# RG-LRU gates: two matmul products in place of three, on operands stacked by 64-channel block

## The chip, the cores and the metric

The kernel runs on one core of a Trainium2 chip. The metric is the device time of one execution in microseconds; of several runs the median is taken.

## The reference

One layer of a diffusion backbone: 1024 latent tokens and 256 context tokens of width 1024. A norm and one wide projection feed two branches, a bidirectional RG-LRU and a bidirectional mLSTM; they are projected, gated, merged and added to the stream, and a SwiGLU layer and a last norm follow. The change touches only the RG-LRU's gates. Each direction d has two of them, r (weights `wa`) and i (weights `wx`), made by 16 blocks of 64 x 64 on the 1024 channels:

```python
def _rglru_coeffs(xc, wa, ba, wx, bx, lam):
    r = jax.nn.sigmoid(_block_diag(xc, wa) + ba).astype(jnp.float32)
    i = jax.nn.sigmoid(_block_diag(xc, wx) + bx).astype(jnp.float32)
    log_a = -RG_C * jax.nn.softplus(-lam.astype(jnp.float32)) * r
    a = jnp.exp(log_a)
    b = jnp.sqrt(-jnp.expm1(2.0 * log_a)) * (i * xc.astype(jnp.float32))
    return a, b
```

`xc` is the projection after a convolution of four taps over the tokens. A linear scan with a and b follows, forward and backward.

## The kernel before

Channels lie on the 128 partitions, tokens in columns. Matmul operands are float32 numbers split into a high part (rounded to fp32r) and the rest, the low part, and each product is made as three matmuls: high x high, high x low, low x high (`gemm`, L107 to 117).

The RG-LRU stage (L671 to 831) handles the channels in eight tiles of 128, that is two blocks of 64 each. A step of its loop (m = 0 to 7) does three things on TensorE: the projection of the next tile m+1 in eight pieces A[0] to A[7] (one per 128 input channels, nine matmuls each, two of 512 latent columns and one of 256 context columns per product), the four gates of tile m (`gate`, L724), and the projection of m's gelu branch (48 matmuls of 512 columns). In the last step there is no next tile, and the pieces belong to a side projection without context columns (six matmuls each).

A gate q = 2d + j (direction d; j = 0 for r, 1 for i) has 128 x 128 weights with its two blocks on the diagonal and zeros elsewhere. It is made on 1284 columns (256 context, three of padding between, 1024 latent, one more), cut into 512, 512 and 260, each with three matmuls into the accumulator tile `pt`. There is one such tile (`bufs=1`, three banks), so the next gate waits until ScalarE has read it: one sigmoid over 128 partitions x 1284 columns (L734).

The rest of a step, in the order in which the code has it:

- ScalarE: sigmoid and tanh of gate 0, sigmoids of gates 1, 2 and 3, a tanh, copies of the next tile's projection from the accumulators (L687, L688), two roots (L818), two exponentials (L820), rounding of the next tile's high part (`high`, L696), gelu (L827). Tables are loaded ahead of roots, exponentials, gelu and sigmoids.
- VectorE: the `tail` of the tile before (L754: products, scans, sums), two products of i with xc (L796, L804), low parts of weights (L100, L721), the taps (`conv`, L201 and L203), two combinations (L821), the low part of the next tile (`low`, L700).
- GpSimd rounds weights (L97, L720), clears paddings and issues the stores; SP issues the loads.

This order is written out by hand and kept: the loop stands in `tc.manual_schedule(engines=ENG4)` (L779) for TensorE, ScalarE, VectorE and GpSimd, so each of them runs its instructions in the order of the code and stands still where one has to wait. The high part lies in the tile `xh` (one buffer), the low part in a buffer of tag `X` (two). Weights of the gates are packed on the host by `layout`.

Of the kernel before, what the change touches and what calls it, by code (L numbers as in the profile page):

```python
# [17 lines left out]
KT = 8  # L18
EPS = 1e-6
NFF = 22  # L20
LP = 1284
# [21 lines left out]
def hybrid_block(ctx, tc, xT, ctxT, vec, gbias, wmod, wmt, win, wbr, wbm, wo, wfi, wfo, qkvt, wif, rgw,  # L43
# [17 lines left out]
    def V(name, i=0, n=1):  # L61
        o = VEC[name][0] + i
        return vt[:, o:o + n]
# [607 lines left out]
    with pool("p2") as p2, pool("p2t", bufs=1, space=PSUM) as pt_, pool("p2c", bufs=1, space=PSUM) as pc_:  # L671
        PW = 1312

        def wide(tag, bufs, dt=F32, n=LP):
            return p2.tile([128, PW], dt, tag=tag, name=tag, bufs=bufs)[:, 0:n]

        def rg_parts(m, w):

# [15 lines left out]
            def high():  # L694
                got["xh"] = wide("xh", 1, F32R)
                nc.scalar.activation(got["xh"], got["xc"], AF.Identity)  # L696

            def low():
                got["xl"] = wide("X", 2, F32R)
                nc.vector.tensor_tensor(got["xl"], got["xc"], got["xh"].bitcast(F32), op=ALU.subtract)  # L700

# [21 lines left out]

        def gate(m, q, got, rhl):  # L724

            d, j = q // 2, q % 2
            (rh, rl), xh, xl = rhl, got["xh"], got["xl"]
            pt = pt_.tile([128, 1536], F32, tag="gt", name="pt")
            for a, b in ((0, 512), (512, 1024), (1024, LP)):
                nc.tensor.matmul(pt[:, a:b], lhsT=rh[:, q], rhs=xh[:, a:b], start=True, stop=False)  # L730
                nc.tensor.matmul(pt[:, a:b], lhsT=rh[:, q], rhs=xl[:, a:b], start=False, stop=False)
                nc.tensor.matmul(pt[:, a:b], lhsT=rl[:, q], rhs=xh[:, a:b], start=False, stop=True)
            g = wide(f"g{j}", 4)
            nc.scalar.activation(g, pt[:, 0:LP], AF.Sigmoid, bias=V(("ba", "bx")[j], 8 * d + m))  # L734
            return g

        def half_tanh(m, d, r):

            t = wide("t", 3)
            nc.scalar.activation(t, r, AF.Tanh, scale=hsp[:, 8 * d + m:8 * d + m + 1])  # L740
            return t
# [37 lines left out]
        with tc.manual_schedule(engines=ENG4):  # L779
            for m in range(KT):  # L780
# [3 lines left out]
                else:  # L784
                    A, store = side_parts(nw)
                r, t, ii = [None] * 2, [None] * 2, [None] * 2
                A[0]()
                A[1]()
                if before:
                    tail(*before)  # L790
                r[0] = gate(m, 0, got, rhl)
                t[0] = half_tanh(m, 0, r[0])
                A[2]()
                A[3]()
                ii[0] = gate(m, 1, got, rhl)
                nc.vector.tensor_tensor(ii[0], ii[0], got["xc"], op=ALU.mult)  # L796
                w = load_split(win[8 + m])
                A[4]()
                A[5]()
                r[1] = gate(m, 2, got, rhl)  # L800
                A[6]()
                ii[1] = gate(m, 3, got, rhl)
                t[1] = half_tanh(m, 1, r[1])
                nc.vector.tensor_tensor(ii[1], ii[1], got["xc"], op=ALU.mult)  # L804
                if more:
# [741 lines left out]
def layout(inputs):  # L1547
# [38 lines left out]
    for j, n in enumerate(("ml_wi", "ml_wf")):  # L1586
        for d in range(2):
            o = 8 * j + 4 * d
            wif[:, :, :, o:o + 4] = f[n][0, d].reshape(3, KT, 128, 4).transpose(2, 0, 1, 3)
    rgw = np.zeros((128, KT, 4, 128), np.float32)  # L1590
    for d in range(2):
        for j, n in enumerate(("rg_wa", "rg_wx")):
            w = f[n][0, d].reshape(KT, 2, 64, 64)
            for b in range(2):
                rgw[64 * b:64 * b + 64, :, 2 * d + j, 64 * b:64 * b + 64] = w[:, b].transpose(1, 0, 2)
    s = np.arange(128)
# [40 lines left out]
```

## Time and profile before

| what | value |
|---|---|
| median of 3 runs | 1857.31 us (1856.84 to 1858.59) |
| the profiled execution | 1857.61 us, span 1855.8 us |
| TensorE busy | 1828.0 us, 98% of the span |
| TensorE weight loads | 1511.5 us, 81% |
| VectorE busy | 1191.1 us, 64% |
| ScalarE busy | 631.1 us, 34% |
| GpSimd busy | 325.0 us, 18% |
| mean granted TensorE clock | 0.997 |
| chain that ended last | 93% TensorE, 5% VectorE, 1% ScalarE, 1% issue |

The profile is one execution taken by the hardware profiler. The span runs from the first to the last instruction. An engine's idle time in front of an instruction is given in brackets with what ended it. Matmuls overlap in their records, so how long a group of them takes is read from start to start. The RG-LRU stage begins at about 225 us and its loop ends at about 480.

### The profile page before, as it was taken

The page shows a single profiled execution, that of the slowest core. Times are in us where ns is not written, and L with a number is a line of the kernel's source. Part 1 is how long each engine was busy: PE and PEld are TensorE (multiplying, and loading weights), DVE is VectorE, ACT ScalarE, POOL GpSimd, SP SyncE. Part 2 cuts the span into 40 slices and gives each one's busy share as a digit, 9 for nine tenths or more (in the row PEclk, how much of TensorE's full clock was granted, in tenths as well). Part 3 has the DMA queues.
Part 4 walks back from the last instruction along what each step waited for, and adds up shares of the span by engine and source line. Part 5 has one row for each costly group of instructions (what it writes and reads, how often), then busy time and mean ns, then how long its engine had stood idle before and what let it go on. Part 6 is the DMA issues. An engine that isn't in the chain of part 4 may idle for free.

```text
span 1855.8 us, 22833 instructions
## 1 busy us (share of the span) xinstructions
PE 1828.0 (98%) x8850; PEld 1511.5 (81%) x8850; DVE 1191.1 (64%) x1717; ACT 631.1 (34%) x902; POOL 325.0 (18%) x444
## 2 busy tenths in 40 slices
PE   7899999999999999999999999999999999999997
PEld 5778788888888888888888888888888888888887
DVE  6875669889526363636676446787855555687756
ACT  5432357576333232323200012543333333210013
POOL 1121110110134343434101022110000000110003
PEclk9999999999999999999999999999999999999999
DMA  8242211111543333332786443343422222642102
GB/s 349 84 154 94 84 52 57 52 65 50 187 111 73 121 85 109 88 106 79 282 320 215 138 158 136 137 148 131 156 83 80 85 75 108 243 168 99 57 1 91
DMA packets 89364, 227.75 MB, mean 123 GB/s; under 512 B 8073, under 2 KB 37289, under 8 KB 89129
## 3 DMA queue, kind: packets, MB, share of 16 engines
q1 hardware_dynamic: 75864, 179.74, 29.1%
q0 software_dynamic: 12688, 46.17, 6.5%
q8 instruction: 69, 1.13, 0.3%
q10 hardware_dynamic: 704, 0.40, 0.1%
q14 instruction: 39, 0.31, 0.1%
HBM read 175.85 MB, written 50.43 MB: 122 GB/s over the span
## 4 chain that ended last, share of the span: by engine, by line
PE 93%; DVE 5%; ACT 1%; issue 1%; DMA 0%; SPq 0%; POOL 0%; DVEq 0%; ACTq 0%
PE pg L115 12%; PE pg L113 12%; PE pg L117 12%; PE pp L1179 7%; PE pp L1181 7%; PE pp L1180 7%; PE pp L1457 4%; PE pp L1459 4%; PE pp L1458 4%; PE pC L957 3%; PE po L951 2%; PE po L113 2%; PE po L115 2%; PE po L117 2%; PE po L949 1%; PE pt L730 1%
## 5 line engine op out<-in xcount | busy, mean ns | idle before, releaser
L115 PE MATMUL pg<-al,wh 128*128 128x512 f32 x896 | 281.9, 395 | 5.3 <-DVE al L362 3.5
L113 PE MATMUL pg<-ah,wh 128*128 128x512 f32 x896 | 282.8, 396 | 2.9 <-ACT ah L340 1.7
L117 PE MATMUL pg<-ah,wl 128*128 128x512 f32 x896 | 279.5, 393 | 0.0
L97 POOL TENSOR_SCALAR wh<-wr 128x1024 fp32r<-128x1024 f32 x102 | 112.2, 1103 | 614.8 <-PE pg L115 222.5
L100 DVE TENSOR_TENSOR wl<-wr,wh 128x1024 fp32r<-128x1024 f32 x102 | 126.6, 1243 | 120.8 <-POOL wh L97 120.1
L115 PEld LDWEIGHTS pg<-al,wh 128*128 128x128 f32 x896 | 164.3, 189 | 40.3 <-DVE al L362 3.9
L117 PEld LDWEIGHTS pg<-ah,wl 128*128 128x128 f32 x896 | 165.0, 189 | 33.9
L113 PEld LDWEIGHTS pg<-ah,wh 128*128 128x128 f32 x896 | 162.7, 189 | 35.7 <-issue 4.5
L1457 PE MATMUL pp<-hh,wh 128*128 128x512 f32 (+1 forms) x384 | 144.4, 376 | 0.0
L1458 PE MATMUL pp<-hh,wh 128*128 128x512 f32 (+1 forms) x384 | 144.1, 375 | 0.0
L1459 PE MATMUL pp<-hh,wl 128*128 128x512 f32 (+1 forms) x384 | 144.1, 375 | 0.0
L1471 DVE SCALAR_TENSOR_TENSOR xs<-pp,g,xs 128x512 f32<-128x512 f32 x144 | 105.5, 746 | 48.0 <-PE pp L1459 45.3
L1179 PE MATMUL pp<-th,oh 128*128 128x512 f32 x264 | 102.8, 389 | 0.0
L1181 PE MATMUL pp<-th,ol 128*128 128x512 f32 x264 | 102.7, 389 | 0.0
L1180 PE MATMUL pp<-tl,oh 128*128 128x512 f32 x264 | 102.7, 389 | 0.0
L1191 DVE TENSOR_TENSOR c<-c,pp 128x512 f32<-128x512 f32 x84 | 57.4, 683 | 69.5 <-PE pp L1181 52.1
L1226 ACT ACTIVATE oh<-os 128x512 fp32r<-128x512 f32 x88 | 55.3, 632 | 133.1 <-PE pp L1180 103.1
L962 DVE SCALAR_TENSOR_TENSOR Cn<-Cn,decs,pC 128x257 f32<-128x257 f32 x128 | 57.6, 477 | 46.6 <-PE pC L957 46.6
L1405 POOL DMA_DIRECT2D s_h<-c x44 | 23.9, 543 | 361.8 <-DVE c L1404 338.3
L1459 PEld LDWEIGHTS pp<-hh,wl 128*128 128x128 f32 x384 | 72.3, 188 | 14.0
L1457 PEld LDWEIGHTS pp<-hh,wh 128*128 128x128 f32 x384 | 72.3, 188 | 13.9
L1458 PEld LDWEIGHTS pp<-hh,wh 128*128 128x128 f32 x384 | 72.3, 188 | 13.9
(350 smaller groups left out, 3754.1 us busy)
## 6 DMA issues: line engine op xcount, KB each, us to landing
wr<-in_wfi SPq DMA_DIRECT2D x53, 512.0 KB, 3.4
wr<-in_win SPq DMA_DIRECT2D x48, 512.0 KB, 3.4
wr<-in_wmt SPq DMA_DIRECT2D x32, 512.0 KB, 4.8
s_h<-c POOLq DMA_DIRECT2D x44, 256.0 KB, 2.5
wr<-in_wfo SPq DMA_DIRECT2D x22, 512.0 KB, 4.3
g<-s_h SPq DMA_DIRECT2D x22, 512.0 KB, 4.6
wm<-in_wmod SPq DMA_DIRECT2D x16, 512.0 KB, 7.9
wr<-in_wo SPq DMA_DIRECT2D x16, 512.0 KB, 3.4
```

The lines of the kernel that those rows point to most:

```text
L97: nc.gpsimd.tensor_scalar(h, r, 1.0, 0.0, op0=ALU.mult, op1=ALU.add)
L100: nc.vector.tensor_tensor(l, r, h.bitcast(F32), op=ALU.subtract)
L113: nc.tensor.matmul(o, lhsT=wh[:, k], rhs=h(k), start=f, stop=False)
L115: nc.tensor.matmul(o, lhsT=wh[:, k], rhs=l(k), start=False, stop=False)
L117: nc.tensor.matmul(o, lhsT=wl[:, k], rhs=h(k), start=False, stop=e)
L1179: nc.tensor.matmul(o, lhsT=wh(k), rhs=bh(k), start=new and k == 0, stop=False, skip_group_check=True)
L1180: nc.tensor.matmul(o, lhsT=wh(k), rhs=bl(k), start=False, stop=False, skip_group_check=True)
L1181: nc.tensor.matmul(o, lhsT=wl(k), rhs=bh(k), start=False, stop=not more and k == n - 1, skip_group_check=True)
L1457: nc.tensor.matmul(po, lhsT=wh[:, m], rhs=hh[:, sl], start=i == 0, stop=False)
L1458: nc.tensor.matmul(po, lhsT=wh[:, m], rhs=hl[:, sl], start=False, stop=False)
L1459: nc.tensor.matmul(po, lhsT=wl[:, m], rhs=hh[:, sl], start=False, stop=i == n - 1)
L1471: nc.vector.scalar_tensor_tensor(xs[:, m, sls[t]], po, g2[:, m:m + 1], xs[:, m, sls[t]], op0=ALU.mult, op1=ALU.add)
```

## The change

For each block b of a tile one operand z[b] of 128 partitions is made: the block's 64 channels in their high part on the block's own partitions, and the same 64 channels in their low part on the other 64. `high` and `low` therefore write two half tiles each, in place of one whole tile; a half of `low` reads the partitions of one block and writes those of the other.

The weights are packed anew: for direction d and block b, both halves of the 128 rows hold the same 64 x 64 weights, `wa` in columns 0 to 63 and `wx` in 64 to 127. One matmul with the high part of these weights thus adds the products with the high and with the low part of the block, and a second one with the low part of the weights adds the rest (and low x low, which was left out before). A call of `gates(m, d, b)` makes r and i of one block with six matmuls, in place of nine for one gate of two blocks. r is on partitions 0 to 63 of `pt` and i on 64 to 127, so each call is read by two sigmoids of 64 partitions x 1284 columns.

There are still four such calls in a step. They stand after A[0], A[2], A[4] and A[6] now; the four gates stood after A[1], A[3], A[5] and A[6]. The first tanh, the first product with xc and the load of the gelu weights follow the second call.

```diff
@@ -674,6 +674,8 @@
         def wide(tag, bufs, dt=F32, n=LP):
             return p2.tile([128, PW], dt, tag=tag, name=tag, bufs=bufs)[:, 0:n]
 
+        BLK = [(0, slice(0, 64)), (1, slice(64, 128))]
+
         def rg_parts(m, w):
 
             pg = pg_.tile([128, 2, 512], F32, tag="g", name="pg")
@@ -692,12 +694,15 @@
                 conv(got["xc"], got["X"], "rgcw", "rgcb", m)
 
             def high():
-                got["xh"] = wide("xh", 1, F32R)
-                nc.scalar.activation(got["xh"], got["xc"], AF.Identity)
+
+                got["z"] = [wide("xh", 1, F32R), wide("X", 2, F32R)]
+                for b, o in BLK:
+                    nc.scalar.activation(got["z"][b][o], got["xc"][o], AF.Identity)
 
             def low():
-                got["xl"] = wide("X", 2, F32R)
-                nc.vector.tensor_tensor(got["xl"], got["xc"], got["xh"].bitcast(F32), op=ALU.subtract)
+                for b, o in BLK:
+                    z = got["z"][b]
+                    nc.vector.tensor_tensor(z[BLK[1 - b][1]], got["xc"][o], z[o].bitcast(F32), op=ALU.subtract)
 
             return [lambda k=k: gemm(w, movs, [k]) for k in range(KT)], copies, taps, high, low, got
 
@@ -721,18 +726,17 @@
             nc.vector.tensor_tensor(rl, rw, rh.bitcast(F32), op=ALU.subtract)
             return rh, rl
 
-        def gate(m, q, got, rhl):
-
-            d, j = q // 2, q % 2
-            (rh, rl), xh, xl = rhl, got["xh"], got["xl"]
+        def gates(m, d, b, got, rhl, outs):
+
+            (rh, rl), z, o = rhl, got["z"][b], BLK[b][1]
             pt = pt_.tile([128, 1536], F32, tag="gt", name="pt")
-            for a, b in ((0, 512), (512, 1024), (1024, LP)):
-                nc.tensor.matmul(pt[:, a:b], lhsT=rh[:, q], rhs=xh[:, a:b], start=True, stop=False)
-                nc.tensor.matmul(pt[:, a:b], lhsT=rh[:, q], rhs=xl[:, a:b], start=False, stop=False)
-                nc.tensor.matmul(pt[:, a:b], lhsT=rl[:, q], rhs=xh[:, a:b], start=False, stop=True)
-            g = wide(f"g{j}", 4)
-            nc.scalar.activation(g, pt[:, 0:LP], AF.Sigmoid, bias=V(("ba", "bx")[j], 8 * d + m))
-            return g
+            for a, e in ((0, 512), (512, 1024), (1024, LP)):
+                nc.tensor.matmul(pt[:, a:e], lhsT=rh[:, 2 * d + b], rhs=z[:, a:e], start=True, stop=False)
+                nc.tensor.matmul(pt[:, a:e], lhsT=rl[:, 2 * d + b], rhs=z[:, a:e], start=False, stop=True)
+            for j in range(2):
+                if b == 0:
+                    outs.append(wide(f"g{j}", 4))
+                nc.scalar.activation(outs[j][o], pt[BLK[j][1], 0:LP], AF.Sigmoid, bias=V(("ba", "bx")[j], 8 * d + m)[o])
 
         def half_tanh(m, d, r):
 
@@ -783,25 +787,26 @@
                     A, copies, taps, high, low, ngot = rg_parts(m + 1, nw)
                 else:
                     A, store = side_parts(nw)
-                r, t, ii = [None] * 2, [None] * 2, [None] * 2
+                gg, t = ([], []), [None] * 2
                 A[0]()
-                A[1]()
                 if before:
                     tail(*before)
-                r[0] = gate(m, 0, got, rhl)
-                t[0] = half_tanh(m, 0, r[0])
+                gates(m, 0, 0, got, rhl, gg[0])
+                A[1]()
                 A[2]()
+                gates(m, 0, 1, got, rhl, gg[0])
+                t[0] = half_tanh(m, 0, gg[0][0])
+                nc.vector.tensor_tensor(gg[0][1], gg[0][1], got["xc"], op=ALU.mult)
+                w = load_split(win[8 + m])
                 A[3]()
-                ii[0] = gate(m, 1, got, rhl)
-                nc.vector.tensor_tensor(ii[0], ii[0], got["xc"], op=ALU.mult)
-                w = load_split(win[8 + m])
                 A[4]()
+                gates(m, 1, 0, got, rhl, gg[1])
                 A[5]()
-                r[1] = gate(m, 2, got, rhl)
                 A[6]()
-                ii[1] = gate(m, 3, got, rhl)
-                t[1] = half_tanh(m, 1, r[1])
-                nc.vector.tensor_tensor(ii[1], ii[1], got["xc"], op=ALU.mult)
+                gates(m, 1, 1, got, rhl, gg[1])
+                t[1] = half_tanh(m, 1, gg[1][0])
+                nc.vector.tensor_tensor(gg[1][1], gg[1][1], got["xc"], op=ALU.mult)
+                r, ii = [g[0] for g in gg], [g[1] for g in gg]
                 if more:
                     rhl = rg_weights(m + 1)
                 A[7]()
@@ -1587,12 +1592,13 @@
         for d in range(2):
             o = 8 * j + 4 * d
             wif[:, :, :, o:o + 4] = f[n][0, d].reshape(3, KT, 128, 4).transpose(2, 0, 1, 3)
+
     rgw = np.zeros((128, KT, 4, 128), np.float32)
     for d in range(2):
         for j, n in enumerate(("rg_wa", "rg_wx")):
-            w = f[n][0, d].reshape(KT, 2, 64, 64)
-            for b in range(2):
-                rgw[64 * b:64 * b + 64, :, 2 * d + j, 64 * b:64 * b + 64] = w[:, b].transpose(1, 0, 2)
+            w = f[n][0, d].reshape(KT, 2, 64, 64).transpose(2, 0, 1, 3)
+            for h in range(2):
+                rgw[64 * h:64 * h + 64, :, 2 * d:2 * d + 2, 64 * j:64 * j + 64] = w
     s = np.arange(128)
     masks = np.zeros((128, 2, 128), np.float32)
     masks[:, 0] = np.where(s[:, None] <= s[None, :], 0.0, NEG)
```

## Rows read from the trace of the kernel before

**Rows 1.** The page, part 1: busy time of each engine, share of the span, instructions.

```profile
PE 1828.0 (98%) x8850; PEld 1511.5 (81%) x8850; DVE 1191.1 (64%) x1717; ACT 631.1 (34%) x902; POOL 325.0 (18%) x444
```

**Rows 2.** Windows, the RG-LRU stage: stretch, length, busy time by engine, clock, DMA, GB/s.

```profile
400.00:430.00 30.00, 30.00 (x149) 25.27 (x148) 25.93 (x19) 21.54 (x18) 3.47 (x7) 1.00 0.17 62
```

**Rows 3.** Timeline, ScalarE, one steady step: start, length, line, operation, idle before it.

```profile
404.37 1.33 ACT L734 ACTIVATE g<-pt,vt 128x1284 f32<-128x1284 f32 x1 [2.16 <-PE pt L732]
405.60 1.36 ACT L740 ACTIVATE t<-g,hsp 128x1284 f32<-128x1284 f32 x1
...
415.73 1.26 ACT L696 ACTIVATE xh<-xc 128x1284 fp32r<-128x1284 f32 x1
417.01 1.28 ACT L827 ACT_TABLE_LOAD   x1
...
419.35 1.28 ACT L734 ACT_TABLE_LOAD   x1
422.26 1.33 ACT L734 ACTIVATE g<-pt,vt 128x1284 f32<-128x1284 f32 x1 [1.62 <-PE pt L732]
...
436.24 1.34 ACT L734 ACTIVATE g<-pt,vt 128x1284 f32<-128x1284 f32 x1 [2.16 <-PE pt L732]
```

**Rows 4.** Timeline, TensorE, same step: gate 0, the two A pieces, gate 1.

```profile
420.31 0.40 PE L730 MATMUL pt<-xh,rh 128*128 128x512 f32 x1
...
422.06 0.62 PE L113 MATMUL pg<-ah,wh 128*128 128x512 f32 x2
...
425.54 0.40 PE L730 MATMUL pt<-xh,rh 128*128 128x512 f32 x1
```

**Rows 5.** Timeline, VectorE: three scans of different partitions and columns.

```profile
209.38 0.42 DVE L605 TENSOR_TENSOR_SCAN bcum<-ones,LF 64x128 f32<-64x128 f32 x1
...
421.13 0.69 DVE L751 TENSOR_TENSOR_SCAN g<-g,g 128x256 f32<-128x256 f32 x1
421.86 2.35 DVE L752 TENSOR_TENSOR_SCAN g<-g,g 128x1024 f32<-128x1024 f32 x1
```

**Rows 6.** Timeline, all engines: TensorE starts again after a wait for ScalarE.

```profile
87.32 0.38 ACT L538 ACTIVATE X<-pc 128x256 f32<-128x256 f32 x1 [3.15 <-DVE shw L537]
...
87.75 0.39 PE L113 MATMUL pc<-ch,wh 128*128 128x258 f32 x1 [0.67 <-ACT X L538]
...
87.97 0.28 PE L115 MATMUL pc<-cl,wh 128*128 128x258 f32 x1
...
88.10 0.28 PE L117 MATMUL pc<-ch,wl 128*128 128x258 f32 x1
```

**Rows 7.** Timeline, VectorE, the same steady step.

```profile
405.73 2.29 DVE L804 TENSOR_TENSOR g<-g,xc 128x1284 f32<-128x1284 f32 x1 [2.74 <-ACT g L734]
...
418.20 1.49 DVE L700 TENSOR_TENSOR X<-xc,xh 128x1284 fp32r<-128x1284 f32 x1
419.61 1.49 DVE L746 TENSOR_TENSOR g<-t,g 128x1284 f32<-128x1284 f32 x1
...
433.64 1.23 DVE L100 TENSOR_TENSOR wl<-wr,wh 128x1024 fp32r<-128x1024 f32 x1 [0.94 <-POOL wh L97]
```

**Rows 8.** Timeline, ScalarE, the last step (m=7).

```profile
453.52 1.34 ACT L734 ACTIVATE g<-pt,vt 128x1284 f32<-128x1284 f32 x1 [1.00 <-PE pt L732]
...
458.04 1.33 ACT L734 ACTIVATE g<-pt,vt 128x1284 f32<-128x1284 f32 x1 [1.78 <-PE pt L732]
...
466.00 1.34 ACT L734 ACTIVATE g<-pt,vt 128x1284 f32<-128x1284 f32 x1 [2.12 <-PE pt L732]
```

**Rows 9.** Timeline, VectorE and TensorE, just ahead of the first step.

```profile
224.57 1.11 DVE L640 TENSOR_SCALAR dgd<-ident,ae 128x128 f32<-128x128 f32 x1
...
225.73 0.49 PE L644 MATMUL pcol<-dgd,ones 128*128 128x128 f32 x2 [0.40 <-DVE dgd L640]
```

**Rows 10.** Timeline of TensorE and windows, after its long wait near the start.

```profile
63.76 0.91 PE L115 MATMUL pg<-al,wh 128*128 128x512 f32 x2 [3.49 <-DVE al L362]
...
64.00:68.00 4.00, 4.00 (x12) 3.13 (x12) 4.00 (x5) 1.15 (x1) 0.00 (x0) 0.57 0.11 1
```

## The prediction

> **What bounds the kernel now.** I read the page's busy shares first: TensorE is busy 98% of the span, VectorE 64%, ScalarE 34% [rows 1]. So TensorE time that is removed counts, as long as nothing else takes its place where it is removed. The changed code lies in the RG-LRU stage, some 225 to 470 us into the span, so I then read the busy time of that stage: in 30 us TensorE has 30.00, VectorE 25.93, ScalarE 21.54, clock 1.00 [rows 2]. TensorE is the bound there and nothing waits on its side, but VectorE has only 4 us of room in 30 and ScalarE 8. The change takes from the first and gives to the other two, so the rest is a question of order, read from the timelines of one steady step (m=5 to m=6; the eight steps repeat it).
>
> I put time zero at the start of the step's last sigmoid, 404.37 us, and the next step's last sigmoid is at 436.24: a step is 31.87 us [rows 3].
>
> **TensorE's part.** One gate is nine matmuls from 420.31 to 422.06, 1.75 us [rows 4]. After the change one call has six of the same forms (two thirds of each), 1.75 x 2/3 = 1.167 us. Four calls a step save 4 x 0.583 = 2.33 us, eight steps 18.7 us. Two A pieces (one k each of the next tile's projection) lie between 422.06 and 425.54: 3.48 us, 1.74 for one. Were TensorE alone the bound, a step would be 29.54 us and the kernel 18.7 us faster.
>
> **What the half tiles add.** Each step gains four sigmoids and one rounding (high) on ScalarE and one subtraction (low) on VectorE, each instruction now over 64 partitions and the same 1284 columns. The trace has no 64-partition instruction of these forms. Bounds: half of the whole one's time if cost went by area, and the whole one's time if it goes by columns. The nearest rows are VectorE's scans: 64 partitions x 128 columns take 0.42, 128 x 256 take 0.69 and 128 x 1024 take 2.35 [rows 5]; the line through the last two, (2.35 - 0.69)/768 = 2.16 ns a column, gives 0.41 for 128 columns on 128 partitions. Half the partitions saved nothing there, so I take the whole time for every half.
>
> The Trainium skill (ScalarE: Activation LUTs, section "What ACT_TABLE_LOAD costs") prices an ACTIVATE at about 280 ns + 0.833 ns per column, with no term for partitions. That would be an estimate of 1.35 us for a half sigmoid; the whole one shows 1.33, and no row here has a half. By it the sum below stays as it is, and it speaks against the change.
>
> **ScalarE's way around the step.** Its order is written out by hand, so it is a chain: last sigmoid, tanh, two copies, table, two roots, table, two exponentials, high, table, gelu, table, first sigmoid. Before: from 404.37 to the end of the last table load, 419.35 + 1.28 = 420.63, is 16.26 us; then it idles 1.62 for TensorE [rows 3]. After the change the chain begins with two sigmoids, one more at a pitch of 405.60 - 404.37 = 1.23, and has one more high at 417.01 - 415.73 = 1.28. The first sigmoid of the next step can start at 16.26 + 1.23 + 1.28 = 18.77, the second half at 20.00, and it ends at 21.33. There is one accumulator tile (pt, bufs=1), so the second call of the next step can't start on TensorE until both halves are read: 21.33 + 0.05, where 0.05 is what passed from a ScalarE end (87.70) to TensorE's start (87.75) [rows 6].
>
> **VectorE's way to the same point.** It too is fixed by hand: the last product waits for the last sigmoid, then weights, taps, weights, two combinations, low. Everything up to low starts 1.23 later, as the last half sigmoid ends 1.23 later, and neither the copies nor the exponentials get nearer, since they shift alike. Low started at 418.20, 13.83 after zero [rows 7]; the first half's now starts at 15.06, takes 1.49 and ends at 16.55. The first call needs it: 16.60. TensorE is there much earlier: before, it came to the gate at 420.31 - 404.37 = 15.94, behind two A pieces; now only A[0] is ahead of it, 15.94 - 1.74 = 14.20. So it stands still 2.40 us at the first call, and in order behind this wait are A[1], A[2] and all the rest. A restart costs 0.10 more: after a wait the next matmul started 0.22 later (87.75, 87.97), without one 0.13 (87.97, 88.10) [rows 6]. TensorE then reaches the second call at 16.60 + 0.10 + 1.167 + 3.48 = 21.35. Both ways meet within 0.03: 21.35 and 21.38. (Sigmoid 1 could start at 17.87 + 0.20 for the matmul's end, earlier than 18.77, so ScalarE doesn't wait.)
>
> **The step after.** From 21.38: three calls and two pairs of A, 3 x 1.167 + 2 x 3.48 = 10.46, and 422.26 - 422.06 = 0.20 to the sigmoid [rows 3, 4]: 32.04 us against 31.87, +0.17. The 2.33 us saved come back as 2.50 of waiting. Six such steps (m=1 to 6): +1.0 us.
>
> The last step (m=7) has shorter A pieces: its first two sigmoids are 4.52 apart, so a pair is 4.52 - 1.75 = 2.77, and the step took 466.00 - 436.24 = 29.76 [rows 3, 8]. After: the second call at 21.38 + 0.10; from call to call TensorE needs 1.167 + 2.77 = 3.94, while pt comes free after 1.167 + 0.20 + 1.23 + 1.33 + 0.05 = 3.98, so twice 3.98, then 1.167 + 0.20: 30.81, +1.05.
>
> The first step (m=0) has no chain ahead of it and keeps its 2.33. But before the loop the second low is one more VectorE instruction, about 1.4 us, ahead of the diagonal (L640, 224.57) for which TensorE already waits 0.40 at 225.73 [rows 9]. Bounds 0 (placed behind it) and 2.7 (high counted too); I take 1.4: -0.9.
>
> **Edits costed at nothing.** Weights wl for the gelu projection: they now stand on VectorE behind two lows and the tail. The tail with its last product starts at 419.61, wl ended at 433.64 + 1.23 = 434.87, 30.50 after zero [rows 7]; both lows push it by 1.23 + 1.40 = 2.63 to 33.13. The projection starts at 32.04 - 0.20 + 1.74 = 33.58 and uses wl 0.9 later (four matmuls of about 0.23). Cover 1.3 us, before some 4; in the last step, 1.23 shorter, it is missed by about 0.3, which I add. SP's load and GpSimd's copy of these weights move along and end before wl. Gate buffers (4 deep), t and gs come free half a step earlier. Layout of rgw costs nothing: same bytes, same load. After m=7 TensorE goes on with projections that need none of this.
>
> **Sum.** -0.9 + 1.0 + 1.05 + 0.3 = +1.45 us. The profiled execution took 1857.61 (span 1855.8 and 1.8 around it), so 1859.1; the median of the runs shown is 0.3 lower, 1857.31, and gives 1858.8.
>
> The Trainium skill (VectorE: DVE Perf Modes, section "Two Vector instructions with no wait between them") holds a Vector instruction whose operands start in another quadrant than the last one's until that is finished. The rows show 0.08 of overlap (1.49 long, 1.41 to the next start, 418.20 to 419.61) that the first low would lose; by the rule a step would be 0.05 longer and the sum 0.3 more. No row here has such a pair.
>
> **Rivals.** A change within 0.2%, 3.7 us, I count as none; this is about what can be told apart.
>
> *Faster: halves are cheaper.* If area counts, two halves cost one whole: ScalarE's pair takes 1.33 in all and nothing shifts by 1.23. Low starts at 13.83, its first half ends at 14.58, the second call comes at 14.63 + 0.10 + 1.167 + 3.48 = 19.38, pt is free at 16.26 + 1.33 = 17.59. The step is 19.38 + 10.46 + 0.20 = 30.04, -1.83; seven of them and -0.9: -13.7, 1843.6. It can't get under 1838.6 (all 18.7). Against it stand the scans [rows 5].
>
> *Slower: low into the other half is dearer.* It reads one half of the partitions and writes the other, which nothing in the trace does. Its end sets TensorE's start, with 0.03 us to spare. At 2.29, the dearest two-input product of this size (L804) [rows 7], it adds 0.77 x 6 = +4.6, 1863.4; at twice the time (2.98) 1.46 x 6 + 0.7 = +9.5, 1868.3. From 1.9 us on (3.7 - 1.45 over six steps, on 1.49) the change is slower by over 0.2%. Any hidden 0.4 us on ScalarE's halves does the same.
>
> *Slower: the clock.* After TensorE had idled 3.49 us (to 63.76) the granted clock was 0.57 over the next 4 us, 1.7 us lost; after one of 0.67 (87.75) the matmuls kept their short time, 0.28 [rows 6, 10]. The wait of 2.4 lies between. Seven such losses are +12: 1870.8.
>
> *It does not do what it says:* excluded, the diff drops a third of the gate matmuls.
>
> **How the numbers follow.** Forecast (halves cost the same) 0.58, its own range 1855 to 1863: bounds 0 and 2.7 before the loop, 0.3 us either way on each of seven handovers. Of it 0.54 is no change, 0.04 slower. Cheaper halves 0.16, faster. Dearer low or hidden latencies 0.22: 0.21 slower, 0.01 no change. Clock 0.04, slower. So 0.16, 0.55, 0.29. The range, 1848 to 1867, leaves out the greater half of the faster case and the clock.
>
> **What would show it.** Right: gate matmuls 288 to 192; the stage's end about where it was; TensorE waiting some 2.4 us before the first call for low, little before the second; ScalarE without idle time from the last sigmoid to the first of the next step; half sigmoids of 1.33 and lows of 1.49. Wrong: half sigmoids near 0.7, steps near 29.5 us, waits elsewhere than at the first two calls, or a granted clock under 1.00 in the stage.

## The result and the profile after

1877.86 us median of 4 runs (1876.83 to 1879.59); the kernel before, run beside it, 1857.34. The ratio is 1.0108, with an interval of 1.0096 to 1.0121: 20.5 us slower, where 1858.8 was forecast with a range up to 1867. The profiled execution has a span of 1875.9 us against 1855.8, +20.1, and a granted clock of 0.990 against 0.997.

First the page of the changed kernel, part 1, which answers to [rows 1].

```profile
PE 1823.6 (97%) x8754; PEld 1504.1 (80%) x8754; DVE 1199.7 (64%) x1725; ACT 685.0 (37%) x942; POOL 325.6 (17%) x444
```

The 96 matmuls are gone, ScalarE has 40 instructions and 54 us more. TensorE is busy for only 4.4 us less: part of what the fewer matmuls saved was spent in matmuls that took longer.

Next a step of the kernel before and two steps of the changed kernel by windows, cut at the second tanh of a step: stretch, length, busy time of TensorE, its weight loads, VectorE, ScalarE and GpSimd, granted clock, DMA share, GB/s. Below them stands TensorE's wait before the first call in each of the two.

```profile
373.73:405.60 31.87, 31.87 (x158) 26.84 (x157) 27.73 (x20) 21.55 (x20) 3.74 (x7) 1.00 0.17 59
...
350.13:383.99 33.86, 31.38 (x146) 26.02 (x145) 28.70 (x21) 28.36 (x24) 3.42 (x7) 0.95 0.15 55
383.99:416.73 32.74, 30.09 (x146) 24.83 (x145) 28.70 (x21) 28.37 (x23) 4.42 (x7) 1.00 0.14 47
```

```profile
364.25 0.50 PE L734 MATMUL pt<-xh,rh 128*128 128x512 f32 x1 [2.48 <-DVE xh L705]
...
398.10 0.50 PE L734 MATMUL pt<-xh,rh 128*128 128x512 f32 x1 [2.48 <-DVE xh L705]
...
403.21 0.50 PE L734 MATMUL pt<-X,rh 128*128 128x512 f32 x1 [0.17 <-ACT g L739]
```

The two steps do the same work and TensorE waits 2.48 us for the first low half in both; before the second call it waits 0.17. In one the mean granted clock is 0.95 and it lasts 33.86 us, in the other it is 1.00 and it lasts 32.74. Of the six steps m=1 to 6 only this one kept its clock; the five others took 33.70 to 34.20. Before, all took 31.87.

Where the clock goes shows in TensorE's timeline of the step after those (start, length, line, operation, idle time before it and what ended it), and in windows of the same place.

```profile
428.08 0.28 PE L117 MATMUL pc<-ch,wl 128*128 128x256 f32 x1
430.86 0.79 PE L734 MATMUL pt<-xh,rh 128*128 128x512 f32 x1 [2.50 <-DVE xh L705]
431.45 0.63 PE L735 MATMUL pt<-xh,rl 128*128 128x512 f32 x1
...
437.26 0.39 PE L735 MATMUL pt<-X,rl 128*128 128x512 f32 x1
```

```profile
428.00:430.00 2.00, 0.36 (x3) 0.04 (x1) 1.97 (x2) 1.96 (x3) 0.00 (x0) 1.00 0.56 213
430.00:432.00 2.00, 1.14 (x3) 0.95 (x4) 1.97 (x2) 1.97 (x3) 0.00 (x0) 0.63 0.00 0
432.00:434.00 2.00, 2.00 (x8) 1.65 (x7) 1.94 (x3) 1.81 (x2) 0.00 (x0) 0.52 0.00 0
434.00:436.00 2.00, 2.00 (x12) 1.73 (x11) 1.97 (x2) 1.99 (x2) 0.00 (x0) 1.00 0.00 0
```

TensorE stands still for 2.50 us until the first low half is there. Then the granted clock is down to about a half (1.2 GHz in place of 2.4) until 434: the second matmul takes 0.63 us, the same form later in the step 0.39.

ScalarE in the step that kept its clock answers to [rows 3]; the first line is the page's group of all half sigmoids, with its busy time and the mean ns of one.

```profile
L739 ACT ACTIVATE g<-pt,vt 64x1284 f32<-64x1284 f32 x64 | 85.1, 1329 | 42.1 <-PE pt L735 41.2
...
381.28 2.68 ACT L739 ACTIVATE g<-pt,vt 64x1284 f32<-64x1284 f32 x2 [1.99 <-PE pt L735]
383.99 1.37 ACT L744 ACTIVATE t<-g,hsp 128x1284 f32<-128x1284 f32 x1
385.38 0.39 ACT L689 ACTIVATE X<-pc 128x256 f32<-128x256 f32 x1
...
399.19 1.28 ACT L739 ACT_TABLE_LOAD   x1
400.49 2.68 ACT L739 ACTIVATE g<-pt,vt 64x1284 f32<-64x1284 f32 x2
404.68 2.69 ACT L739 ACTIVATE g<-pt,vt 64x1284 f32<-64x1284 f32 x2 [1.52 <-PE pt L735]
```

No idle time stands from 381.28 to 403.17, as forecast; but a half takes 1.33 and a pair 2.68, so the second half starts 1.35 after the first, and the first sigmoid comes 19.21 after the last pair's start, where 18.77 was worked out.

Last the place behind the stage, which the prediction dismissed: ScalarE, then TensorE, in the changed kernel, and the same window of the kernel before and of the changed one.

```profile
529.64 1.28 ACT L890 ACT_TABLE_LOAD   x1 [14.67 <-DMA SW<-s_row]
530.94 2.16 ACT L890 ACTIVATE SW<-SW,cols 128x128 f32<-128x128 f32 x7
537.54 0.40 ACT L890 ACTIVATE SW<-SW,cols 128x128 f32<-128x128 f32 x1 [4.44 <-DVE SW L888]
537.85 1.00 ACT L663 ACTIVATE t<-pg 128x1024 f32<-128x1024 f32 x1
```

```profile
539.00 0.70 PE L113 MATMUL pg<-ah,wh 128*128 128x512 f32 x2 [3.33 <-ACT t L663]
```

```profile
520.00:540.00 20.00, 20.00 (x90) 16.57 (x89) 3.34 (x3) 4.17 (x10) 2.67 (x3) 1.00 0.46 164
...
520.00:540.00 20.00, 16.67 (x74) 13.52 (x73) 3.72 (x5) 5.90 (x15) 1.87 (x3) 0.99 0.81 206
```

The next stage's ScalarE work waits for a transfer, a half tanh stands in order behind eight exponentials, and TensorE waits 3.33 us for that tanh, which frees its accumulator. Before, TensorE had no idle time in this stretch (20.00 busy of 20.00).

By the start of the last pair of sigmoids in a step (as the prediction counts) the +20.1 us are: first step +0.57, six steps +10.92, last step +2.43, behind it +6.2 (1875.9 - 479.92 = 1396.0 against 1389.8). Of the 6.2, 1.5 is only the second half of that last pair; from the second half tanh of the last step on, the loss is 4.7 (1393.3 against 1388.6).

### The profile page after: what moved, and what is told of

Same layout as the page of the kernel before. It is cut to its first block, busy times and chain, and to the rows that moved or that the text cites. A ratio compares the mean times of both kernels' runs of the same rounds, so it can differ in the third digit from the quotient of the medians.

```text
span 1875.9 us, 22712 instructions
## 1 busy us (share of the span) xinstructions
PE 1823.6 (97%) x8754; PEld 1504.1 (80%) x8754; DVE 1199.7 (64%) x1725; ACT 685.0 (37%) x942; POOL 325.6 (17%) x444
## 3 DMA queue, kind: packets, MB, share of 16 engines
q8 instruction: 69, 1.13, 0.3%
## 5 line engine op out<-in xcount | busy, mean ns | idle before, releaser
L739 ACT ACTIVATE g<-pt,vt 64x1284 f32<-64x1284 f32 x64 | 85.1, 1329 | 42.1 <-PE pt L735 41.2
L1463 PEld LDWEIGHTS pp<-hh,wh 128*128 128x128 f32 x384 | 72.4, 188 | 14.0
```

Of the source, the lines that this page charges most:

```text
L1463: nc.tensor.matmul(po, lhsT=wh[:, m], rhs=hl[:, sl], start=False, stop=False)
```

## The experiments

The theory drawn from this profile: (1) the wait before the first call drops the clock; (2) ScalarE's half tiles make a longer chain than worked out; (3) transfers that start later behind the stage. Each run stands beside the kernel before on the same chip, which took 1858.0 to 1858.9 us; losses are given against that.

**e1_fill: the wait filled with useless products.**

```
+            for _ in range(fill):
+                nc.tensor.matmul(pt[:, 0:512], lhsT=rh[:, 2 * d + b], rhs=uh[:, 0, 0:512], start=True, stop=True)
...
-                gates(m, 0, 0, got, rhl, gg[0])
+                gates(m, 0, 0, got, rhl, gg[0], fill=8 if m else 0)
```

> The changed kernel with eight useless matmuls of 512 columns (1.86 us) put in front of the first gate call of steps 1 to 7, on data that is long there, into the accumulator that the gate overwrites. Theory 1 (the wait of 2.5 us for low drops the clock, and the low clock costs time): the wait falls to some 0.6 us, the granted clock stays 1.00 in the stage, steps go from 33.8 to about 32.7 us (ScalarE's way around), the kernel from 1877.9 to about 1870, though it does more work. Theory 2 (the time is lost on ScalarE and VectorE alone, the low clock is hidden behind them): steps stay 33.8, 1877.9 or a little more.

1869.08 us, ratio 1.0053 (1.0037 to 1.0070): a loss of 10.2 us in place of 20.5, although TensorE does more. One step by windows, and the wait left in it:

```profile
317.93:350.68 32.75, 31.95 (x154) 26.28 (x153) 28.70 (x21) 28.36 (x24) 4.51 (x8) 1.00 0.18 61
```

```profile
332.04 0.50 PE L736 MATMUL pt<-xh,rh 128*128 128x512 f32 x1 [0.63 <-DVE xh L705]
```

The low half ends when it did, TensorE waits for it 0.63 us beside the useless work, the clock is 1.00, and all six steps are 32.74 to 32.79, the length of the one step of the changed kernel that kept its clock. So the fall is caused by TensorE's own standing still, and 0.87 a step over 31.87 remains when it is gone. By its places the trace accounts for 6.8 of the 10.3 us regained (5.6 in the six steps, 0.4 in the last, 0.8 behind); the other 3.5 I could not place. This profiled execution was the slowest of the four (1875.11) and started the stage 4 us late: far ahead of the edited code, from 42 to 48 us, its granted clock is 0.50, and between 40 and 60 us it is 0.83 where the changed kernel has 1.00.

**e2_tanh_first: the half tanhs behind the stage planned ahead of the exponentials.**

```
+        with tc.high_priority(offset=100):
-        gate_out(4)
+            gate_out(4)
...
```

> The changed kernel, with the four side projections behind the stage (gate_out(4)) given priority over the mLSTM head's work in the order that is planned at build time, so that the tanh that frees their accumulator stands before the head's exponentials on ScalarE. Theory 3 (6.2 us are lost behind the stage because that tanh stands behind an exponential that waits for a load): the wait of 3.3 us at 539 and the low clock after it go, from the last sigmoid to the end it takes about 1390 us as before, 1872 in all. Rival (the loads' late start holds it wherever the tanh stands): the wait comes back a few us later, 1876 to 1878.

One run: 1875.35 us, span 1873.6, close to the rival's 1876. The 3.3 us wait is gone; waits of 0.29, 0.21 and 1.25 us stand elsewhere in its place, and from the second half tanh of the last step to the end it takes 1391.8, only 1.5 less. So ScalarE's order alone is the smaller part of this term, as far as one run tells. In one step of this run the granted clock stayed at 0.50 from 294 to 300 us, and that step took 35.36.

**e3_whole_sigmoid: half tiles taken away.** One sigmoid over 128 partitions per call in place of two over 64. It leaves out the sorting of r and i into their own tiles, so only its time is of use.

```
-                nc.scalar.activation(outs[j][o], pt[BLK[j][1], 0:LP], AF.Sigmoid, ...[o])
+                if j == b:
+                    nc.scalar.activation(outs[j], pt[:, 0:LP], AF.Sigmoid, ...)
```

> The changed kernel with one sigmoid over all 128 partitions per call in place of two halves: one of the two gates is left out and r and i of different blocks are mixed. Everything else stays. If the half sigmoids on ScalarE are what uses up the saving: low comes 1.3 us earlier, TensorE waits about 1.1 us for it, the clock holds 1.00, a step is about 30.8 us, in all about 1850. If the two halves of low alone hold it: steps stay near 32 or above with the clock low, 1865 or more.

One run: 1855.0 us, span 1853.1, where 1850 was expected.

```profile
370.37:401.73 31.36, 29.81 (x146) 24.84 (x145) 29.88 (x22) 22.71 (x20) 4.11 (x7) 1.00 0.18 59
```

Steps of 31.24 to 31.36 once under way (30.8 expected), the last 29.01, waits for low of 1.13 to 1.81 us, clock 1.00. With whole sigmoids two products gain 0.6 us a step, not the 2.33 that TensorE gives up: VectorE's low is late in any case. Its order behind the stage is that of the kernel before, which ties the new order to the half sigmoids.

**e4_gate_places: the gate calls where they stood before** (behind A1, A3, A5 and A6), the products and half tiles as changed.

```
                 A[0]()
+                A[1]()
                 gates(m, 0, 0, got, rhl, gg[0])
-                A[1]()
                 A[2]()
+                A[3]()        (and so on)
```

> The changed kernel with the four calls (and the tail, product and load between them) at the places of the four gates before: behind A[1], A[3], A[5] and A[6]. Theory 1 (clock): one more A piece covers the wait for low, 2.5 - 1.74 = 0.75 us are left, the clock stays 1.00; between the last two calls TensorE waits some 1.2 us for the accumulator; a step is about 32.2 us, in all about 1867 (the 6 us behind the stage stay). Theory 2 (no cost of the clock): steps of 33.2 or more, 1874 or more.

1866.28 us, ratio 1.0040 (1.0025 to 1.0055).

```profile
342.79:375.08 32.29, 30.41 (x146) 24.84 (x145) 29.10 (x21) 28.36 (x24) 3.78 (x7) 1.00 0.17 57
```

A second A piece now covers most of the wait: TensorE waits 0.7 us for low, 0.2 and 1.0 for sigmoids; the clock is 1.00 and the steps are 32.25 to 32.29. The loss is 7.4 us in place of 20.5: the move of the calls, a part of the change that removes nothing, cost 13.

**e5_places_and_loads: e4 with SyncE's order of before behind the stage.**

```
+        with tc.manual_schedule(engines={SP}):
+            gate_out(4)
+            tm = [tanh_tile(0)]
+            nc.sync.dma_start(masks, masks_d)
+            nc.sync.dma_start(G, s_G)
+            tm.append(tanh_tile(1))
+            ld = loads(0)          # xa, vv, SW, Sb
...
```

> The gate calls stand after A1, A3, A5 and A6, as before the change, and SyncE's order at the head of the next stage is forced back to that of the kernel before (seven weight loads, masks, G, the eighth weight load, then xa, vv, SW and Sb). Theory: the late transfers behind the stage cost the changed kernel 6.2 us there (1396.0 us from the last sigmoid to the end, 1389.8 before); with the old order this comes back to 1389.5 to 1391, and the time is 1866.3 - 6 = 1860 us (1859 to 1862), within 2 us of the kernel before, the steps still being 32.25 us. Rival: the 6 us come from ScalarE's own order or from the later state that the stage hands over, and the time stays at 1865 to 1867 us with 1395 us behind the last sigmoid.

1861.85 us, ratio 1.0017 (1.0008 to 1.0026), 4.4 less than e4. SyncE's queue in the changed kernel, then in e5:

```profile
447.65 62.30 SPq L95 DMA_DIRECT2D wr<-in_win  x7
510.00 0.72 SPq L849 DMA_DIRECT2D masks<-in_masks  x1
...
520.02 3.58 SPq L866 DMA_DIRECT2D SW<-s_row  x1
```

```profile
442.10 45.19 SPq L95 DMA_DIRECT2D wr<-in_win  x5
487.33 0.42 SPq L1028 DMA_DIRECT2D masks<-in_masks  x1
...
498.76 0.33 SPq L95 DMA_DIRECT2D wr<-in_win  x1
...
507.20 3.75 SPq L864 DMA_DIRECT2D SW<-s_row  x1
```

In the changed kernel the masks and all that follows stand in one queue behind a weight load that has to wait for a buffer. Counted from the second half tanh of the last step, the masks are issued after 27.4 us there (510.00 - 482.62), 15.6 in e5; SW after 37.4 and 35.4. TensorE has no idle time from 480 to 560 in e5, and from that tanh to the end it takes 1387.1 us, against 1392.4 in e4 and 1388.6 before: the whole term is back. ScalarE's planned order changed along with it (two exponentials ahead of the third tanh, where the changed kernel has eight), so the two are not taken apart in full; e2, which changed that order alone, got back 1.5.

**e7_halves_alone: the kernel before, with three products, and only its sigmoids cut in halves.**

```
-            nc.scalar.activation(g, pt[:, 0:LP], AF.Sigmoid, bias=...)
+            for o in (slice(0, 64), slice(64, 128)):
+                nc.scalar.activation(g[o], pt[o, 0:LP], AF.Sigmoid, bias=...[o])
```

> The kernel before with three products as it was, and only its sigmoids cut into two half tiles of 64 partitions. Theory: halves cost as much as whole tiles and do not overlap, so ScalarE gets 4 x 1.45 us more per step; TensorE waits 0.9 us before the fourth gate call, and ScalarE's loop with the longer products between the sigmoids comes to 33 us (32.7 to 33.4); the order planned behind the stage changes with it (eight weight loads first) and costs some 6 us there. Time 1859 + 7 x 1.2 + 6 = 1873 us (1870 to 1876). So the products alone would be worth about -0.8 us a step and the halves +1.2. Rival: half tiles are hidden under TensorE in this kernel (ScalarE is busy for 21.6 of 31.9 us): steps of 31.9 us, 1859 to 1865 us, and the changed kernel's loss lies in the new place of the calls alone.

1880.21 us, ratio 1.0118 (1.0098 to 1.0138), 7 us over the expectation and as slow as the whole change.

```profile
347.01 2.67 ACT L735 ACTIVATE g<-pt,vt 64x1284 f32<-64x1284 f32 x2 [2.11 <-PE pt L732]
...
365.54 2.67 ACT L735 ACTIVATE g<-pt,vt 64x1284 f32<-64x1284 f32 x2 [0.63 <-PE pt L732]
...
380.81 2.67 ACT L735 ACTIVATE g<-pt,vt 64x1284 f32<-64x1284 f32 x2 [2.11 <-PE pt L732]
```

Steps of 33.80, +1.93 for halves alone, with the clock at 1.00; I had expected +1.2, and where the other 0.7 comes from I did not find. The order behind the stage changed with them: TensorE waits 4.02 us at 541.39, and from the second half tanh to the end it takes 1393.5. With e4 (same places, two products, 32.26) the products, with the half highs and lows that they need, are worth 1.5 a step in the company of half sigmoids. So the products gain and the half sigmoids lose more.

**e6, e8, e9, e10: the high and low parts made ahead of the combinations**, so that TensorE need not wait, all with e5's order behind the stage and the gate places of the change.

```
                     taps()
+                    high()    # e6: both halves on GpSimd; e8: VectorE and GpSimd; e9, e10: VectorE
+                    low()
                 ...  (roots, exponentials, combinations)
-                    high()
-                    low()
...
```

The cut leaves out that e8 to e10 also move the splits of weights and put the copies of X ahead of the second tanh, and that e10 puts the store of gs behind a split.

> The changed kernel with its gate places as changed, the high part made on GpSimd in place of ScalarE, the high and low parts made directly after the taps and the next weights' split (ahead of the two combinations), and SyncE's old order behind the stage. Theory: with ScalarE's loop 2.5 us shorter and the parts there before TensorE asks, a step is set by TensorE's own products, 30.3 us (32.27 less the 1.9 us of waits that the step with the old places still has), at most 30.8; the granted clock stays 1.00; the time is 1860 - 7 x 1.6 = 1849 us (1846 to 1853), faster than the kernel before. Rival: the GpSimd copy holds VectorE up (or ends too late), the low part comes no earlier and a step is 31.5 us or more: 1856 us or more.

> As e6, with the four things mended that its trace shows in TensorE's way: the split of the side product's weights is issued before the tail of the step before (in e6 its GpSimd half stood behind the store of gs, and TensorE waited 1.3 to 4.0 us for it, after which the granted clock fell), the copies of X go ahead of the second half tanh on ScalarE, the high part of block 0 is made on VectorE and that of block 1 on GpSimd at the same time, and the low part of block 0 goes ahead of the split of the next weights. Theory: TensorE waits under 0.5 us anywhere in a step, the granted clock stays 1.00, and a step is TensorE's own work of 30.3 us or VectorE's of 29.3 us with the GpSimd copies beside it, so 30.3 to 31.0 us; with e5's order behind the stage the time is 1861.9 - 7 x 1.4 = 1852 us (1848 to 1856), under the kernel before. Rival: GpSimd beside VectorE stretches VectorE's work past 31 us, or another wait of 1.3 us or more turns up ahead of a call and the clock falls again: 1859 us or more.

> As e8 with both high parts on VectorE, so that no GpSimd copy stands beside them. Theory: VectorE has 28.4 + 1.9 = 30.3 us of work a step, as much as TensorE; steps of 30.4 to 31.2 us, 1850 to 1857 us. If the GpSimd copy in e8 costs VectorE more than the 0.95 us that it saves there, e9 is the faster of the two; if it costs less, the slower by up to 7 us.

> As e9 (both high parts on VectorE, made with the low parts directly behind the taps), with the split of the next weights ahead of the taps in place of behind the first low part (TensorE waited 2.0 to 3.1 us for it in e8 and e9, ahead of the third product of the step's first piece, and the granted clock fell in five of six steps), and with the store of gs behind that split on GpSimd. Theory: VectorE then has about 30.5 us of work a step, with the calls' operands there at most 1 us after TensorE asks; no wait reaches 1.5 us, the clock stays 1.00, steps are 30.5 to 31.3 us, and the time is 1861.9 - 7 x 1.35 = 1852.4 us (1849 to 1857), under the kernel before. Rival: the low part comes 1.5 to 2.5 us late instead (the split delays the taps), the clock falls again and the steps are 32 us or more: 1859 us or more.

All four missed. e6: 1871.81 us (1.0072, 1.0056 to 1.0089); the low parts were there, but the split of a weight stood behind a store on GpSimd's queue, TensorE waited 1.3 to 2.3 us for it in the six steps, and the clock fell in four of them. e8: 1865.94 (1.0042, 1.0026 to 1.0059) and e9: 1864.84 (1.0039, 1.0023 to 1.0054): that was mended, and now the split of the next weights, which I had put behind the first low part, came 2.0 to 3.1 us late; the clock fell in five of the six steps. e10: 1860.50 (1.0012, 1.0002 to 1.0022), where steps alternate:

```profile
312.06:343.22 31.16, 29.82 (x145) 24.84 (x144) 30.55 (x23) 25.91 (x22) 3.60 (x8) 1.00 0.18 59
343.22:377.36 34.14, 31.35 (x145) 26.05 (x144) 33.52 (x25) 25.91 (x21) 5.77 (x8) 0.95 0.16 54
```

```profile
323.69 0.50 PE L734 MATMUL pt<-xh,rh 128*128 128x512 f32 x1 [1.34 <-DVE xh L705]
356.31 0.56 PE L734 MATMUL pt<-xh,rh 128*128 128x512 f32 x1 [2.79 <-DVE xh L705]
```

One kernel shows both: after a wait of 1.34 us the clock stays, after one of 2.79 us at the same place it falls, and that step is 3.0 us longer. But VectorE is nearly full in both steps (30.55 of 31.16 us, 33.52 of 34.14), so the difference can't be put down to the clock.

**e11 and e12: e10 with the wait filled** (five useless matmuls), **or with e4's places.**

> As e10, with five useless matmuls of 512 columns (1.1 us) ahead of the first gate call of steps 1 to 7. In e10 the steps alternate: TensorE waits 1.34 us before the first call with the clock held (31.16 us) or 2.79 us with the clock falling (34.1 us). Theory: the useless products leave waits of at most 1.7 us, the clock stays 1.00 in every step, all steps are 30.7 to 31.4 us, and the time is 1860.5 - 3 x 3.0 = 1851.5 us (1848 to 1855), under the kernel before although TensorE does more. Rival: the long steps come from VectorE (its taps took 5.66 in place of 4.82 us there) and stay over 32.5 us without a lower clock: 1857 us or more.

> As e10, with the gate calls after A1, A3, A5 and A6, as before the change. Theory: the first call comes 1.75 us later, so TensorE waits at most 1.1 us there and about 1.0 us before the fourth call for the sigmoids (as in e4); the clock stays 1.00, and a step is 29.8 + 1.0 to 1.6 us of waits, 30.8 to 31.5 us; time 1861.9 - 7 x 1.1 = 1854 us (1850 to 1857). Rival: the later calls delay the fourth pair of sigmoids and with it the copies and the taps by as much, so that the wait comes back and the steps are 32 us as in e5: 1860 to 1863 us.

e11: 1860.05 us (1.0009, 0.9999 to 1.0018). e12: 1859.05 (1.0004, 0.9994 to 1.0013). Both as long as the kernel before. The clock held in all six steps, yet they settled at 32.63 and 32.25, as the rivals of both had it. A late step of e11:

```profile
341.92:374.55 32.63, 31.01 (x150) 25.71 (x149) 32.02 (x24) 25.92 (x21) 3.61 (x7) 1.00 0.17 57
```

The mean of e10's two steps is 32.65, so holding the clock gained nothing a step: VectorE, busy for 32.02 of 32.63 us here and for 64.07 of the 65.30 of e10's pair, is what both have in common.

**e13 and e14**, to close the sum and to see what holds e12. e13 is the changed kernel with e1's filler and e5's order; e14 is e12 with the high part of block 1 on ScalarE.

> The changed kernel with its own gate places, with e1's eight useless matmuls (clock held) and with SyncE's old order behind the stage. Theory: the two causes add up: 1869.1 (e1) less the 4.4 that the old order was worth in e5 (1866.3 to 1861.9) gives 1864.7 us (1863 to 1866.5), steps of 32.75 us, 1387 to 1388.5 us from the last half tanh to the end; what then is left of the loss, some 6 us against the kernel before, is ScalarE's longer way in six steps (0.87 each, 5.2). Rival: the order behind the stage cost only where the gate places were the old ones; 1868 us or more.

> As e12, with the high part of block 1 on ScalarE behind the exponentials (1.28 us there) in place of VectorE (0.83 us). Theory: VectorE, busy for 31.6 of the 32.25 us of a step in e12, sets the step; with 0.8 us less the step is 31.4 to 31.6 us, the waits for low before the first call become 0.4 us, and the time is 1859.0 - 6 x 0.75 = 1854.5 us (1853 to 1856.5), under the kernel before by 0.2%. Rival: TensorE's 30.1 us and its two waits make the step by the chain through the sigmoids, and taking work from VectorE changes nothing: 32.2 us a step, 1858 to 1861 us.

e13: 1864.84 us (1.0032, 1.0022 to 1.0043), steps 32.73 to 32.78. e14: 1854.68 us (0.9980, 0.9970 to 0.9989), faster than both kernels. A late step of e12, then of e14:

```profile
373.97:406.23 32.26, 30.08 (x145) 24.81 (x144) 31.65 (x24) 25.91 (x22) 4.40 (x7) 1.00 0.18 57
```

```profile
371.91:403.56 31.65, 30.07 (x145) 24.84 (x144) 31.07 (x23) 27.20 (x22) 6.16 (x7) 1.00 0.18 59
```

In e12 VectorE is busy for 31.65 of 32.26 us. Taking 0.8 us from it shortened the step by 0.6 with TensorE's work unchanged: in e12 the bound is VectorE and no longer TensorE. In e14 VectorE is still the fullest engine, 31.07 of 31.65.

## Why the prediction was wrong

What held: the matmuls that go; half tiles that cost as much as whole ones (1.33 for a half sigmoid, 1.49 for a half low, 1.26 for a half high); the wait before the first call, 2.46 to 2.50 in five of the steps m=1 to 6 and 2.82 in m=2, 2.40 worked out; little waiting before the second (0.17); ScalarE without idle time, but for 0.19 in one step. The sum was +1.45 and came out at +20.1. The 18.65 between them, by its own steps:

- **The clock, the step that failed most.** The prediction had the rival (seven losses of 1.7) and its rows: a wait of 3.49 us that brought the clock down, one of 0.67 that did not [rows 6, 10]. It noted that 2.4 lies between, and gave the case 0.04 and nothing in the sum. It fell in six of the seven steps. In the six steps from m=1 on this is 5.7 us (the five slow ones less 32.74 each): about 1.1 net a step, not 1.7; a likely reason, not tested, is that a part of the slower matmuls passes while ScalarE's pair would have held TensorE anyway. e1 regained 10.3 us for it by the medians, of which 6.8 are placed; by the medians this is the largest of the terms. With nothing in the rows to tell which end 2.4 us belongs to, the honest chance was near a half, and the range had to reach beyond 1870.
- **The chain of a step: 32.04 worked out, 32.74 measured, 0.70 in each of six steps, 4.2 us.** A whole sigmoid is followed by the next instruction after 1.23 [rows 3]; I gave halves the same pitch. The pair takes 2.71 to the tanh in place of 2.46, the tanh 1.39 to the copies in place of 1.25, which is nearly all of 19.21 in place of 18.77 to the first sigmoid. Another 0.26 lies between the first pair and the last: the second call starts 2.72 after the first sigmoid in place of 2.61 (403.21 - 400.49), and 0.15 comes behind it. The allowance of 0.3 for a step was too small, since an error here comes back in every step.
- **The last step: +2.43, with 1.35 forecast** (1.05, and 0.3 for a wait on wl that did not come). The clock falls here too, after a wait of 2.86 us, but with the clock held it is still +2.05 (e1, 31.82): 0.4 is the clock's, 0.7 the chain's.
- **"After m=7 TensorE goes on with projections that need none of this": 6.2 us lost there**, 4.7 of it real. The projections need none of it, but the order in which the next stage's transfers are issued is planned at build time from the whole program, and cutting the sigmoids changed it (e7 has the new order, e3 the old one). By their losses e5 against e4 and e13 against e1 price it at 4.4 and 3.9 us.
- **The first step: +0.57, with -0.9 forecast.** VectorE's second low came 2.20 us long ahead of the diagonal (1.49 in the steps; here one of GpSimd's roundings of weights runs beside it, as below), the same place started 1.4 us later to begin with, and the first call, now with one A piece fewer ahead of it, waited 0.94 us for a copy out of the accumulator (decs, L646) that the kernel before had passed by then.

```profile
226.16 2.20 DVE L705 TENSOR_TENSOR X<-xc,X 64x1284 fp32r<-64x1284 f32 x1
...
225.97 1.05 POOL L97 TENSOR_SCALAR wh<-wr 128x1024 fp32r<-128x1024 f32 x1 [12.34 <-issue]
```

On the chip the losses against the kernel before are 20.5 us changed, 10.2 with the clock held (e1), 6.3 with the old order as well (e13). What is left in e13 shows in its trace, whose single execution lost 8.6 of span: first step +2.6, six steps of 32.76 +5.4, last step +2.0 (31.81 against 29.77), behind the stage -1.4.

Two pages were drawn on. By the Trainium skill (ScalarE: Activation LUTs, section "What ACT_TABLE_LOAD costs") the price of an ACTIVATE, given there for 128 partitions, has no term for their number, and the trace agrees: 1.33 for 64 of them, 1.33 for 128 [rows 3]. The same place says that ACTIVATEs back to back overlap by some 93 ns; the whole sigmoid does (1.33 long, 1.23 to the next), the halves do not (1.33 long, 1.35 to the next), and here the measurement decides. By the Trainium skill (VectorE: DVE Perf Modes, section "Two Vector instructions with no wait between them") a Vector instruction whose operands start in another quadrant (a group of 32 partitions) than the last one's is held until that one is done, and the trace agrees for both halves.

```profile
426.38 2.90 DVE L826 SCALAR_TENSOR_TENSOR t<-g,t 128x1284 f32<-128x1284 f32 x2
429.31 1.49 DVE L705 TENSOR_TENSOR xh<-xc,xh 64x1284 fp32r<-64x1284 f32 x1
430.83 1.49 DVE L705 TENSOR_TENSOR X<-xc,X 64x1284 fp32r<-64x1284 f32 x1
```

The first low starts 0.03 after the combinations end (429.28), the second 1.52 after the first for 1.49 of work, where the whole low left 1.41 [rows 7]. That is 0.1 us of VectorE's time each; in the step that kept its clock the second call waits for a sigmoid (0.17, 403.21) and not for a low.

What stays open: why the clock held after 2.48 us in one step (and after 2.47 and 2.48 in e2) and fell after 1.60 in a step of e6; why e7's steps are 0.7 us longer than expected; and why two halves of a tile don't overlap, for which there is no run.

## What to carry to other kernels

Fewer matmuls pay only where TensorE is fed in time; a new wait of 2 us costs itself and, in these traces, mostly a slower clock after it, so keep other work between the last operand and the call that needs it; and see which engine is full before you pay for the clock, since in e11 holding it gained nothing. In these traces cutting an elementwise instruction in two by partitions doubled its cost (1.33 a half, 1.33 the whole); work out a recurring chain by pitches that were seen for that very shape, and multiply the error by the number of steps. When an edit changes durations anywhere, compare the order in which later transfers are issued, since a queue that is in order can hide a buffer wait in front of everything behind it.

## What the runs showed of the hardware

The granted clock of TensorE fell to about a half, for a few us, after most waits of 2 us and more in the stage (28 of 36 in the traces of this case; 2.46 to 2.86: six of seven in the changed kernel; 2.1 to 3.1: five of seven in e8), never after one of up to 1.55 us (1.55 in e3, 1.34 in e10). In between the length of the wait did not decide: it fell after 1.60 (e6), 1.77 (e10) and 1.88 (e12), and held after 1.62 (four times in e11) and 1.81 (e3); 2.48 held once and cost the clock twice in the changed kernel. Half-tile sigmoids followed one another at 1.35 us, whole ones are followed after 1.23. A VectorE product or subtraction of two tiles took 2.20 to 2.29 us in place of 1.49 or 1.50 where one of GpSimd's roundings of weights (1.05 us) had just started beside it (226.16 in the changed kernel; 405.73 in the kernel before, with GpSimd at 405.63). And useless products in a wait made a kernel some 10 us faster.
